# Raw projection weights in two places of their own, and a slab's first down rows loaded when its last pair begins

## The chip, the cores and the metric

The kernel runs on one core of a Trainium2 chip. A core has five engines that run side by side and meet only through semaphores: TensorE (PE in the profile; its weight loads are PEld), VectorE (DVE), ScalarE (ACT), GpSimd (POOL) and SyncE (SP), which here issues all loads and stores. Data moves between the chip's main memory and the on-chip memory (128 partitions) by DMA. The metric is the device time of one execution in microseconds (us). Times are medians of several executions. The profile is one more execution, taken with the hardware profiler.

## What is computed

Two identical layers (DEPTH = 2) over 512 tokens of 1024 channels. Each layer is a gated feed-forward block, a mixer and a second feed-forward block, each followed by a layer norm:

```python
def _swiglu(x, wg, wu, wd):
    return (jax.nn.silu(x @ wg) * (x @ wu)) @ wd
...
    for l in range(DEPTH):
        h = 0.5 * _swiglu(x, ffn_w_gate[l, 0], ffn_w_up[l, 0], ffn_w_down[l, 0])
        x = _layernorm(ALPHA * x + h, ln_g[l, 0], ln_b[l, 0])
        h = _mixer(x, w_in[l], ...)
        x = _layernorm(ALPHA * x + h, ln_g[l, 1], ln_b[l, 1])
        h = 0.5 * _swiglu(x, ffn_w_gate[l, 1], ffn_w_up[l, 1], ffn_w_down[l, 1])
        x = _layernorm(ALPHA * x + h, ln_g[l, 2], ln_b[l, 2])
```

`wg` and `wu` are 1024 x 2816 and `wd` is 2816 x 1024. The mixer projects with `w_in` (1024 x 1792), runs a convolution branch, a recurrent branch and windowed attention, and projects back with `w_out` (1024 x 1024). All in float32.

## The kernel before

**Split numbers.** TensorE is fed float32r values. To keep float32 accuracy every operand is split into a high and a low part (`split`, lines 128 to 132: ScalarE casts the high part at L131, VectorE subtracts it from the source at L132), and every product is three matmuls: low weight by high data, high by low, high by high.

**The feed-forward block** (`ffn`, L465) runs over 22 blocks of 128 hidden channels, two of them making a *pair*, so 11 pairs, in three *slabs* of 4, 4 and 3 pairs (`SLABS`). A pair (class `Pair`, L397) multiplies gate and up weights by the transposed activations in a scheme with seven products instead of eight, so it has seven *steps* named p1, p2, q6, p5, p7, p4 and q3. Each step needs its own combination of the four raw quarters of the pair's weights: `prep` (L428) forms sums t1 to t4 on VectorE (L420) where needed and splits the result. `prep` runs AHEAD = 3 steps in front of the step that is computed. The list `seq` (L551 to L555) puts p4 and q3 of one pair behind p1 of the next, so that after p1 of the last pair of a slab come eight steps: p4 and q3 of the pair before, then p2, q6, p5, p7, p4 and q3 of the last pair. The results end in `hH` and `hL` (`finish`, L492).

When a slab's pairs are done, its *down rows* follow (L578 to L581): for every hidden block f of the slab, `load_rows` loads 128 rows of `wd` (512 KB), splits them, and 24 matmuls of 512 columns (four tiles of tokens, six each, `rowmm`, L454) add to eight PSUM banks. The last slab of a block treats its last four rows (`RESIDENT`) differently: they stay on chip and are used tile by tile in `tail` (L311), which also runs the layer norm (`norm_a`, `norm_b`) and transposes the new activations for the next phase (`to_xT`). So a block has three changes from pairs to down rows, and there are four blocks: twelve changes, four of them in a last slab.

**Places.** A tile pool has a fixed number of places of one tile each, here 128 x 1024 float32. `wpool` has 15 places that serve everything tagged "w": the raw weights that `fetch_raw` (L364) loads, the split halves `wh` and `wl`, the sums t1 to t4, the two result tiles `oa` and `ob` of a pair, and four tiles of the mixer. `load` (L369) asks for raw, high and low, in that order. A raw tile's place comes free when VectorE has subtracted (L132). The pairs' raw quarters (L409) lie in another pool, `tpool`, with 7 places. `fetch_raw` serves the down rows, the mixer's `w_in` and `w_out`, and the first four weight tiles of every block or mixer, which the phase before loads through `nxt.load` (L590 to L592 and in the mixer's end).

**Order.** Tile, the framework, orders the instructions of each engine when the program is built: mostly in program order, but an instruction whose operands and place are there can be put ahead of earlier ones that still wait. Places of one tag are handed out in program order. On the chip every engine then runs its list strictly in order, and SP is one such list: a load whose place is not free holds up every load behind it.

Of the kernel before, what the change touches and what calls it, by code (L numbers as in the profile page):

```python
# [11 lines left out]
F32 = mybir.dt.float32  # L12
# [6 lines left out]
P = 128  # L19
D = 1024  # L20
# [31 lines left out]
def tile_hymba(  # L52
# [26 lines left out]
    nc = tc.nc  # L79

    cpool = ctx.enter_context(tc.tile_pool(name="cpool", bufs=1))
    wpool = ctx.enter_context(tc.tile_pool(name="wpool", bufs=15))
    hpool = ctx.enter_context(tc.tile_pool(name="hpool", bufs=1))
    xpool = ctx.enter_context(tc.tile_pool(name="xpool", bufs=1))
    tpool = ctx.enter_context(tc.tile_pool(name="tpool", bufs=7))
# [6 lines left out]
    def nm(s):  # L92
        uid[0] += 1
        return f"{s}_{uid[0]}"

    def bank():
        return psum.tile([P, 512], F32, tag="ps", name=nm("ps"))
# [36 lines left out]
    def transposed(dst, q, j, src):  # L134

        pt = bank()
        for c in range(4):
            nc.tensor.transpose(pt[:, c * P:(c + 1) * P], src[:, c * P:(c + 1) * P], ident)  # L138
        sl = slice(j * P, j * P + P)
        split(dst[q][:, 0, :, sl], dst[q][:, 1, :, sl], pt.rearrange("p (c t) -> p c t", c=4))  # L140
# [179 lines left out]
    class Start:  # L320
# [6 lines left out]
        def load(self, n=1, pool=None):  # L327
            for _ in range(n):
                self.pairs.append(self.thunks.pop(0)(pool))
# [32 lines left out]
                    mm(pb[:, lo:hi], wh[:, k, :], mh, False, k == KC - 1)  # L362

    def fetch_raw(src):  # L364
        raw = wpool.tile([P, D], F32, tag="w", name=nm("raw"))
        nc.sync.dma_start(raw if len(src.shape) == 2 else raw.rearrange("p (k f) -> p k f", k=KC), src)
        return raw

    def load(src, pool=None, raw=None):  # L369
        raw = fetch_raw(src) if raw is None else raw  # L370
        if pool is None:
            hi = wpool.tile([P, D], F32R, tag="w", name=nm("wh"))
            lo = wpool.tile([P, D], F32R, tag="w", name=nm("wl"))
        else:
            hi = tpool.tile([P, D], F32R, tag="t", name=nm("wh"))
            lo = tpool.tile([P, D], F32R, tag="t", name=nm("wl"))
        split(hi, lo, raw)
        return hi, lo
# [5 lines left out]
        pair = load(cols(src, c), pool, raw)  # L384
        return [w.rearrange("p (k f) -> p k f", k=KC) for w in pair]

    def load_rows(src, c, pool=None):
        return load(src[c * P:(c + 1) * P, :], pool)

# [62 lines left out]
    def rowmm(ys, a, w, first, last):  # L454
        ah, al = a
        wh, wl = w
        for hf in range(2):
            sl = slice(hf * 512, (hf + 1) * 512)
            mm(ys[hf], al, wh[:, sl], first, False)
        for hf in range(2):  # L460
            sl = slice(hf * 512, (hf + 1) * 512)
            mm(ys[hf], ah, wl[:, sl], False, False)
            mm(ys[hf], ah, wh[:, sl], False, last)

    def ffn(l, i, idx, start, nxt, last, hooks={}):  # L465
        wd = w_down[l, i]
# [8 lines left out]
        def product(step, n, pb, first):  # L475
            src, q = A[step]
            wh, wl = pairs[n].ready.pop(step)
            for g in range(2):
                o = pb[:, g * HALF:(g + 1) * HALF]
                for k in range(4):  # L480
                    st = first and g == 0 and k == 0
                    nc.tensor.matmul(o, wl[:, g, k, :], src[q][:, 0, k, :], start=st, stop=False, skip_group_check=True)  # L482
                    nc.tensor.matmul(o, wh[:, g, k, :], src[q][:, 1, k, :], start=False, stop=False, skip_group_check=True)  # L483
                    nc.tensor.matmul(o, wh[:, g, k, :], src[q][:, 0, k, :], start=False, stop=k == 3, skip_group_check=True)  # L484

        for si, (n0, n1) in enumerate(SLABS):
            fin = si == len(SLABS) - 1
            f0, f1 = 2 * n0, 2 * n1
# [3 lines left out]
            def finish(n, which, tile_, s0):  # L492

                v = tile_.rearrange("p (b g s) -> p b g s", b=2, g=2)
                nc.scalar.activation(v[:, :, 0, :], v[:, :, 0, :], AF.Silu)
                nc.vector.tensor_tensor(v[:, :, 0, :], v[:, :, 0, :], v[:, :, 1, :], op=ALU.mult)  # L496
                f = 2 * (n - n0)
                sl = (slice(None), slice(f, f + 2), slice(s0, s0 + HALF))
                split(hH[sl], hL[sl], v[:, :, 0, :])

            def run(step, n):
                if step in ("p1", "p2", "p5"):
                    acc[step, n] = bank()
                pb = acc[{"p1": "p1", "q6": "p1", "p7": "p1", "p4": "p1", "p2": "p2", "p5": "p5", "q3": "p5"}[step], n]
                product(step, n, pb, step in ("p1", "p2", "p5"))
                if step == "p1":
                    outs[n] = [wpool.tile([P, D], F32, tag="w", name=nm("o")) for _ in range(2)]
                oa, ob = outs[n]
                lo, hi = slice(0, 512), slice(512, 1024)
                if step == "p1":  # L510
                    nc.scalar.copy(oa[:, lo], pb)  # L511
                elif step == "p2":
                    nc.vector.tensor_tensor(oa[:, lo], pb, oa[:, lo], op=ALU.add)
                    acc.pop(("p2", n))
                elif step == "q6":
                    nc.scalar.copy(oa[:, hi], pb)
                elif step == "p7":
                    nc.scalar.copy(ob[:, hi], pb)  # L518
                    nc.vector.tensor_tensor(ob[:, hi], acc["p5", n], ob[:, hi], op=ALU.subtract)
                elif step == "p4":  # L520
                    nc.scalar.copy(ob[:, lo], pb)
                    finish(n, 1, ob, HALF)
                elif step == "q3":
                    nc.vector.tensor_tensor(oa[:, hi], pb, oa[:, hi], op=ALU.subtract)
                    finish(n, 0, oa, 0)
                    acc.pop(("p5", n))
                    acc.pop(("p1", n))
                    outs.pop(n)
# [28 lines left out]
            for m, (step, n) in enumerate(seq):  # L557
                while ready < min(len(seq), m + 1 + AHEAD):
                    st, k = seq[ready]
                    pairs[k].prep(st)  # L560
                    ready += 1
                    if st == "p5" and k + 1 < n1:
                        pairs[k + 1].raw(0, 0)
                        pairs[k + 1].raw(1, 0)
                run(step, n)
                if m4:
                    transposed(sT, 2, 2 - len(m4), m4.pop(0))
                if step == "q3" and n in hooks:
                    hooks[n]()
# [4 lines left out]
            def hpair(f, t):  # L574
                return hH[:, f - f0, t * P:(t + 1) * P], hL[:, f - f0, t * P:(t + 1) * P]

            flow = f1 - RESIDENT if fin else f1
            for f in range(f0, flow):  # L578
                w = load_rows(wd, f)
                for t in range(NT):  # L580
                    rowmm(ys[t], hpair(f, t), w, f == f0, f == f1 - 1)  # L581
            if not fin:
# [4 lines left out]
                continue  # L587
            coef = ln_coef(idx)
            ws = [load_rows(wd, f) for f in range(flow, f1)]
            if nxt:  # L590
                nxt.load(3)
# [9 lines left out]
    def mixer(l, idx, start, nxt):  # L601
# [305 lines left out]
        for u in range(U + 2):  # L907
            if u < U:
                scores(u)
            if u < 2:  # L910
                query(2 + u)
            if SLAB_FROM <= u < SLAB_FROM + 4:
                wo.append(load_rows(w_out[l], 4 + u - SLAB_FROM))
            if 0 <= u - 2 < U:
                weighted(u - 2)
            if u - 3 in closes:
                attn_out(closes[u - 3], wo)
            if 0 <= u - 1 < U:
                transpose_p(u - 1)
            point()  # L920
            if u < U:
                normalise(u)
# [7 lines left out]
    for l in range(DEPTH):  # L930
        phases += [(ffn, (l, 0, 3 * l), ffn_start(l, 0)), (mixer, (l, 3 * l + 1), mixer_start(l)),
                   (ffn, (l, 1, 3 * l + 2), ffn_start(l, 1))]
# [61 lines left out]
```

## Time and profile before

| what | us |
|---|---|
| median of 3 executions | 1774.04 (1771.74 to 1775.43) |
| profiled execution, its own time | 1780.14 |
| its span on the core | 1778.4 |
| TensorE busy | 1720.0 (97% of the span) |
| VectorE busy | 1278.1 (72%) |
| ScalarE busy | 821.1 (46%) |
| loads and stores, mean rate | 100 GB/s |
| granted TensorE clock, mean | 0.987 |

Matmuls are pipelined: a matmul's shown duration is longer than its distance to the next one, and its end is modelled. Waits of TensorE are therefore read from the starts of its instructions. In the views of the trace a row of the timeline has the start, the duration, engine, line, operation, written tile and read tiles, and in brackets the engine's idle time before it with what ended it. A row of the waits has the total in us, the number of times and the longest. A row of the windows has the window, its length, each engine's busy time and count, the granted clock, the share of the DMA engines' time and the rate.

### The profile page before, as it was taken

Reading aid. Unit: us, or ns where it says so; the run is one execution under the profiler, and the core shown is the slowest. Engines: PE = TensorE matmul, PEld = TensorE weight load, DVE = VectorE, ACT = ScalarE, POOL = GpSimd, SP = SyncE. Lnnn points to the kernel's source line nnn. Section 1 sums busy time; section 2 is a strip of 40 time slices with the busy share of each in tenths; the row PEclk is TensorE's granted clock in tenths of the full one; section 3 lists DMA queues with packets and bytes.
Section 4 is the critical chain, followed back from the end, with each engine's and each line's share of the span. In section 5 each row is a group of like instructions: output and inputs, shape, how many; then the busy total and the mean of one; then the engine's idle time right before and its main releaser. Section 6 shows DMA issues by size and latency. Waiting matters only on the chain. (4 is left out here: it accounts for less than half of the span.)

```text
span 1778.4 us, 27912 instructions
## 1 busy us (share of the span) xinstructions
PE 1720.0 (97%) x11538; PEld 1546.7 (87%) x11538; DVE 1278.1 (72%) x1777; ACT 821.1 (46%) x1224; POOL 44.0 (2%) x76
## 2 busy tenths in 40 slices
PE   8999999999999999999999999999999999999997
PEld 8988989887679989979889899898875799898896
DVE  5856856779877856747688567576898877577485
ACT  4543533543854543434445335254457445255252
POOL 0200000010000000000000000000000000000000
PEclk9999999999899999999999999999998999999999
DMA  5341542321222432422324324223311244235122
GB/s 157 109 142 57 167 135 72 119 81 45 98 84 75 127 131 72 129 85 72 107 84 131 131 71 128 87 72 110 111 59 58 73 124 144 65 104 163 45 94 72
DMA packets 236840, 177.34 MB, mean 100 GB/s; under 512 B 9524, under 2 KB 219561, under 8 KB 236713
## 3 DMA queue, kind: packets, MB, share of 16 engines
q1 hardware_dynamic: 236712, 175.55, 32.1%
q8 instruction: 91, 1.49, 0.3%
q14 instruction: 37, 0.30, 0.0%
HBM read 171.33 MB, written 3.67 MB: 98 GB/s over the span
## 5 line engine op out<-in xcount | busy, mean ns | idle before, releaser
L132 DVE TENSOR_TENSOR wl<-raw,wh 128x1024 fp32r<-128x1024 f32 x268 | 324.9, 1221 | 156.3 <-ACT wh L131 114.2
L482 PE MATMUL ps<-xT,wl 128*128 128x256 f32 x1280 | 355.5, 278 | 10.8 <-ACT o L518 9.8
L483 PE MATMUL ps<-xT,wh 128*128 128x256 f32 x1280 | 353.3, 276 | 0.0
L484 PE MATMUL ps<-xT,wh 128*128 128x256 f32 x1280 | 353.2, 276 | 0.0
L131 ACT CAST wh<-raw 128x1024 fp32r<-128x1024 f32 x268 | 278.5, 1048 | 132.7 <-DMA raw<-in_ffn_w_down_dram 69.8
L132 DVE TENSOR_TENSOR wl<-t,wh 128x1024 fp32r<-128x1024 f32 x160 | 195.8, 1226 | 143.4 <-ACT wh L131 117.7
L106 PE MATMUL ps<-wl,hH 128*128 128x512 f32 x704 | 276.5, 393 | 4.2 <-DVE wl L132 4.2
L106 PE MATMUL ps<-wh,hH 128*128 128x512 f32 x704 | 275.5, 391 | 0.0
L482 PE MATMUL ps<-sT,wl 128*128 128x256 f32 x960 | 264.8, 276 | 4.9 <-ACT o L511 4.9
L484 PE MATMUL ps<-sT,wh 128*128 128x256 f32 x960 | 264.1, 275 | 0.0
L483 PE MATMUL ps<-sT,wh 128*128 128x256 f32 x960 | 264.1, 275 | 0.0
L131 ACT CAST wh<-t 128x1024 fp32r<-128x1024 f32 x160 | 167.6, 1055 | 201.2 <-DVE t L420 166.0
L482 PEld LDWEIGHTS ps<-xT,wl 128*128 128x128 f32 x1280 | 241.2, 188 | 15.2 <-ACT o L518 12.1
L483 PEld LDWEIGHTS ps<-xT,wh 128*128 128x128 f32 x1280 | 241.3, 188 | 0.3
L484 PEld LDWEIGHTS ps<-xT,wh 128*128 128x128 f32 x1280 | 241.1, 188 | 0.0
L106 PE MATMUL ps<-wh,hL 128*128 128x512 f32 x704 | 218.6, 392 | 4.7 <-ACT wh L131 4.7
L106 PE MATMUL ps<-xT,wh 128*128 128x256 f32 (+1 forms) x960 | 214.3, 318 | 2.2 <-DVE xT L132 2.2
L482 PEld LDWEIGHTS ps<-sT,wl 128*128 128x128 f32 x960 | 180.3, 188 | 6.6 <-ACT o L511 5.8
L484 PEld LDWEIGHTS ps<-sT,wh 128*128 128x128 f32 x960 | 180.2, 188 | 0.0
L483 PEld LDWEIGHTS ps<-sT,wh 128*128 128x128 f32 x960 | 180.2, 188 | 0.0
L106 PEld LDWEIGHTS ps<-xT,wh 128*128 128x128 f32 x960 | 159.2, 191 | 17.1 <-DVE xT L132 3.2
L106 PEld LDWEIGHTS ps<-wl,hH 128*128 128x128 f32 x704 | 132.9, 189 | 35.2 <-DVE wl L132 7.7
(165 smaller groups left out, 2345.7 us busy)
## 6 DMA issues: line engine op xcount, KB each, us to landing
raw<-in_ffn_w_down_dram SPq DMA_DIRECT2D x88, 512.0 KB
raw<-in_ffn_w_gate_dram SPq DMA_DIRECT2D x160, 256.0 KB
raw<-in_ffn_w_up_dram SPq DMA_DIRECT2D x160, 256.0 KB
raw<-in_w_in_dram SPq DMA_DIRECT2D x28, 512.0 KB
raw<-in_w_out_dram SPq DMA_DIRECT2D x16, 512.0 KB
raw<-in_ffn_w_gate_dram SPq DMA_DIRECT2D x8, 512.0 KB
raw<-in_ffn_w_up_dram SPq DMA_DIRECT2D x8, 512.0 KB
t<-in_ln_g_dram SPq DMA_DIRECT2D x6, 512.0 KB
```

What stands on the lines that cost most here:

```text
L106: nc.tensor.matmul(o, a, b, start=start, stop=stop)
L131: nc.scalar.copy(hi, src)
L132: nc.vector.tensor_tensor(lo, src, hi.bitcast(F32), op=ALU.subtract)
L482: nc.tensor.matmul(o, wl[:, g, k, :], src[q][:, 0, k, :], start=st, stop=False, skip_group_check=True)
L483: nc.tensor.matmul(o, wh[:, g, k, :], src[q][:, 1, k, :], start=False, stop=False, skip_group_check=True)
L484: nc.tensor.matmul(o, wh[:, g, k, :], src[q][:, 0, k, :], start=False, stop=k == 3, skip_group_check=True)
```

## The change

Raw weights that `fetch_raw` loads get a pool `rpool` with two places of their own (tag "r"). `wpool` grows from 15 to 16 places and no longer holds them. When a slab's last pair comes to its step p1, the raw tiles of the slab's first two down rows are asked for, before p1's matmuls in program order; `load_rows` takes such a tile where there is one. All other loads keep their place in the program.

```diff
-    wpool = ctx.enter_context(tc.tile_pool(name="wpool", bufs=15))
+    wpool = ctx.enter_context(tc.tile_pool(name="wpool", bufs=16))
+    rpool = ctx.enter_context(tc.tile_pool(name="rpool", bufs=2))
...
     def fetch_raw(src):
-        raw = wpool.tile([P, D], F32, tag="w", name=nm("raw"))
+        raw = rpool.tile([P, D], F32, tag="r", name=nm("raw"))
         nc.sync.dma_start(raw if len(src.shape) == 2 else raw.rearrange("p (k f) -> p k f", k=KC), src)
         return raw
...
-    def load_rows(src, c, pool=None):
-        return load(src[c * P:(c + 1) * P, :], pool)
+    def load_rows(src, c, pool=None, raw=None):
+        return load(src[c * P:(c + 1) * P, :], pool, raw)
...
+                if (step, n) == ("p1", n1 - 1):
+                    first_raw = {f: fetch_raw(wd[f * P:(f + 1) * P, :]) for f in (f0, f0 + 1)}
                 run(step, n)
...
             for f in range(f0, flow):
-                w = load_rows(wd, f)
+                w = load_rows(wd, f, None, first_raw.pop(f, None))
```

## The prediction

> **What bounds the kernel now.** I read the page first, then the waits, then the chain and the timelines around the changes from pairs to down rows.
>
> ```profile
> span 1778.4 us, 27912 instructions
> ...
> PE 1720.0 (97%) x11538; PEld 1546.7 (87%) x11538; DVE 1278.1 (72%) x1777; ACT 821.1 (46%) x1224; POOL 44.0 (2%) x76
> ```
>
> TensorE is the bound, so a change that leaves its matmuls alone can only win what it waits: 58.4 us by these rows (1778.4 - 1720.0), somewhat more by starts, as ends are modelled late. The waits of PE, by what ended them:
>
> ```profile
> PE ps L482 <- ACT o L518: 9.8, 12, 1.7
> PE ps L138 <- DVE xs L306: 6.7, 5, 1.6
> ...
> PE ps L106 <- ACT wh L131: 4.7, 7, 2.1
> PE ps L106 <- DVE wl L132: 4.2, 8, 0.5
> ```
>
> The reader sees four stalls. The first (twelve times, once per slab) is p4 waiting until ScalarE has copied p7's bank. The second is the norm chain ahead of the transposes. The last two, 8.9 us in seven and eight places, are down rows whose weights are not split yet; these the change aims at. The chain at one of them, the second slab of the last block (start, us, what):
>
> ```profile
> 1623.44 2.37 DVE wl L132 x2
> 1625.83 0.37 SPq L412
> ...
> 1626.29 3.75 DMA raw<-in_ffn_w_down_dram
> 1630.06 1.06 ACT wh L131
> 1631.14 1.24 DVE wl L132
> 1632.42 43.37 PE ps L106 x190
> ```
>
> The load of the first down row is issued only at 1626.29, behind a pair load (L412) of the *next* slab that waited in SP's list for VectorE. Then load, cast and subtraction follow one another, 3.75 + 1.06 + 1.24 us, and the pairs' matmuls are over before.
>
> **Term 1: the stall at the change.** In a last slab there is none; compare starts (PE, last pair matmul and first row matmul with a low weight):
>
> ```profile
> 337.67 0.28 PE L484 MATMUL ps<-sT,wh 128*128 128x256 f32 x1
> ...
> 338.25 0.40 PE L106 MATMUL ps<-wl,hH 128*128 128x512 f32 x1
> ```
> ```profile
> 101.39 0.28 PE L484 MATMUL ps<-sT,wh 128*128 128x256 f32 x1
> ...
> 103.80 0.50 PE L106 MATMUL ps<-wl,hH 128*128 128x512 f32 x1 [0.53 <-DVE wl L132]
> ```
> ```profile
> 753.93 0.28 PE L484 MATMUL ps<-sT,wh 128*128 128x256 f32 x1
> 756.31 0.73 PE L106 MATMUL ps<-wh,hL 128*128 128x512 f32 x2 [2.10 <-ACT wh L131]
> 757.57 0.79 PE L106 MATMUL ps<-wl,hH 128*128 128x512 f32 x1 [0.53 <-DVE wl L132]
> ```
> ```profile
> 1630.42 0.28 PE L484 MATMUL ps<-sT,wh 128*128 128x256 f32 x1
> ...
> 1632.42 0.50 PE L106 MATMUL ps<-wl,hH 128*128 128x512 f32 x1 [0.53 <-DVE wl L132]
> ```
>
> The distance is 0.58 us in the last slab and 2.41, 3.64 and 2.00 us in the first, the worst and the last of the eight others; in order the eight are 2.41, 1.84, 1.52, 3.64, 1.70, 2.10, 1.70, 2.00, together 16.9. Less 8 x 0.58 that is **12.3 us**; the wait rows, 8.9, are the lower end.
>
> Does it go? The two raw places are idle through the pairs (pairs load into `tpool`), so nothing on chip holds the two loads back, and SP issues what has a place long before its turn:
>
> ```profile
> 13.95 0.58 SPq L189 DMA_DIRECT2D sink<-in_attn_sinks_dram  x1
> ```
> ```profile
> 189.39 0.31 SPq L180 DMA_DIRECT2D t<-in_conv_dw_w_dram  x1
> ```
>
> Both belong to `load_params`, after pair 5. The one with a place of its own went at 14 us, the other waited for a pool place until 189. So I expect the down loads well ahead of the last pair. Cast and subtraction then need two places of the 16: while q3 is split, at most four split pairs (p5, p7, p4, q3) and `oa`, `ob` are live, 10, so six are free and two rows take four. The nearest rows are those of the last slab, whose raw was early:
>
> ```profile
> 332.04 1.05 ACT L131 CAST wh<-raw 128x1024 fp32r<-128x1024 f32 x1
> ```
> ```profile
> 333.62 1.21 DVE L132 TENSOR_TENSOR wl<-raw,wh 128x1024 fp32r<-128x1024 f32 x1
> ```
>
> Split by 334.83, used at 337.8: 3 us to spare. I take the whole 12.3. What is late next is only L518's wait in each slab, which stays.
>
> **The other down rows** now go through two raw places instead of up to four loads at once. A place turns in about 3.75 + 1.06 + 1.24 = 6.1 us, two places give a row every 3.0 us, and PE takes 43.37 / 190 x 24 = 5.5 us per row. Hidden, at no cost; it would cost from 11 us per turn on.
>
> **Term 2: the norm chain.** At the end of a block four loads for the next phase share places with the resident rows, and their subtractions stand in VectorE's list between the norms:
>
> ```profile
> 883.86 0.69 DVE L290 SCALAR_TENSOR_TENSOR t<-ps,xs 128x512 f32<-128x512 f32 x1 [12.39 <-PE ps L106]
> ...
> 890.96 1.21 DVE L132 TENSOR_TENSOR wl<-raw,wh 128x1024 fp32r<-128x1024 f32 x1
> ```
> ```profile
> 897.21 0.66 PE L138 MATMUL ps<-ident,xs 128*128 128x128 f32 x4 [1.14 <-DVE xs L306]
> ```
> ```profile
> 903.00 0.41 PE L138 MATMUL ps<-ident,xs 128*128 128x128 f32 x2 [1.65 <-DVE xs L306]
> ```
>
> VectorE idles 12.39 us and then does splits while PE waits for xs. With 16 places for split halves, the eight of the four resident rows and the eight of the next four fit without raw tiles among them, so some splits can move into that idle time. Bounds: nothing, and the 6.7 us of the wait row (three waits like that at 897, two like that at 903). I take the first kind, 3 x 1.14 = **3.4 us**: two splits out of the chain cover it, and the third and fourth raw must still wait for the first two to be split.
>
> **Term 3: the mixer.** Its `w_out` splits may be put earlier, into attention, where VectorE and ScalarE are nearly full:
>
> ```profile
> 447.00:486.00 39.00, 35.94 (x147) 22.55 (x147) 34.09 (x105) 33.45 (x96) 0.00 (x0) 0.87 0.33 110
> ```
>
> Here VectorE is busy 34.09 of 39 us. Four of the later splits could enter, at about 1.2 us of VectorE each: at worst 2 mixers x 4 x 1.2 = +9.6 us; two leaving would give about -5. I take 0, as nothing in the program's order there changes. The start of the kernel: its third and fourth loads now wait for a raw place; no wait of PE on weights stands in its rows, so 0.
>
> **Sum.** 12.3 + 3.4 = 15.7. Against the profiled execution (1780.14, span 1778.4) that is 1764.4; that execution lies 6.1 us over the median of 1774.04, so the forecast is **1758.3**.
>
> **The clock.** Right after the worst stall the granted clock is low:
>
> ```profile
> 756.60:763.80 7.20, 6.67 (x17) 4.88 (x17) 6.86 (x9) 5.72 (x8) 0.00 (x0) 0.53 0.66 242
> ```
>
> At 0.53 over 7.2 us, 7.2 x 0.47 = 3.4 us are lost; if the stall is the cause, they go too, and the time is 1754.9. The other stalls of this kind show no such loss, and the median may not have it, so the sum leaves it out. The Trainium skill, "TensorE: Matmul & The Clock Gate", section "Why this matters for your kernels", asks for no idle gap over about 3 us. By that rule 2.3 us would be too short and the sum stays at 1758.3; this row speaks rather against it.
>
> **Rivals.**
> - *Tails stay* (VectorE's list keeps its order): 12.3 alone, 1761.7. For it: the idle 12.39 us was there already and not used.
> - *Attention pays* (term 3 at its worst, tails unchanged): 1774.0 - 12.3 + 9.6 = 1771.3. Against it: `w_out` is needed no earlier.
> - *The change does not do what it says*: the two loads stay behind waiting pair loads in SP's list, or their split halves get no place, and the first row is as late as now: 1774.
> - *Slower: the early loads push back the last pair.* They may be issued just ahead of its raw quarters (0,1) and (1,1), on which t1, t2 and q6 hang:
>
> ```profile
> 1607.79 0.50 SPq L412 DMA_DIRECT2D raw<-in_ffn_w_up_dram  x1
> ```
> ```profile
> 1612.58 1.23 DVE L132 TENSOR_TENSOR wl<-t,wh 128x1024 fp32r<-128x1024 f32 x1 [1.12 <-ACT wh L131]
> ```
> ```profile
> 1615.90 0.28 PE L482 MATMUL ps<-sT,wl 128*128 128x256 f32 x1
> ```
> ```profile
> 1626.00:1630.00 4.00, 4.00 (x38) 4.00 (x37) 0.40 (x1) 0.59 (x1) 0.00 (x0) 1.00 0.76 243
> ```
>
> q6's weights are split at 1613.81 and used at 1615.90: 2.1 us to spare. Two rows are 1.05 MB, at 243 GB/s 4.3 us. From 2.1 us of delay on PE waits; at 4.3 it loses 2.2 us in each of 12 slabs, 26 us: 1774.0 - 12.3 + 26 = 1787.7. The Trainium skill, "DMA: Bandwidth & Descriptors", section "Queues, rings and completion order", says that loads from one issuing engine share one ring per DMA engine, taken in ring order; by that a load in front delays the ones behind in full, which speaks for this rival. Against it: SP's rows above, by which loads with a free place go far earlier.
>
> **Chances.** Forecast 0.36 (1758.3); with the clock as well 0.10 (1754.9); tails stay 0.21 (1761.7); attention pays 0.13 (1771.3); no effect 0.10 (1774); slower 0.10 (1787.7). A measurement here tells 0.2%, 3.5 us, from no change: below 1770.5 is faster. Attention paying falls half on either side, so faster 0.73, same 0.17, slower 0.10. The range goes up to 1774, which leaves out the slower case; its low end has both tail waits (6.7), the clock (3.4) and half of what attention could give (2.5): 1774.0 - 12.3 - 6.7 - 3.4 - 2.5 = 1749.
>
> **What would show it.** Right: at all twelve changes the first low-weight row matmul starts about 0.6 us after the last pair matmul; the waits of L106 on `wh` and `wl` fall from 8.9 us to about nothing; the first down loads stand in SP's list ahead of the last pair's last L412; the wait on xs falls from 6.7 to about 3.3 us. Wrong: new waits of L482 on `wl` in a slab's last pair (the collision), PE waits inside attention over the present ones, or row matmuls after the second that wait for `wh`.

## The result and the profile after

The changed kernel takes 1752.0 us (median of 3, 1749.72 to 1752.65) against 1774.04: the ratio is **0.9869 [0.9855, 0.9883]**, 22 us less. The forecast was 1758.3 with a range from 1749 to 1774. The changed kernel's profiled execution took 1749.72 us, its span is 1747.9. In the changed kernel's lines everything behind `fetch_raw` stands one line lower (L107 for L106, L133 for L132, L483 to L485 for the pairs), the mixer three lower.

From the page, the span and the busy times:

```profile
span 1747.9 us, 27899 instructions
...
PE 1701.4 (97%) x11538; PEld 1540.1 (88%) x11538; DVE 1280.6 (73%) x1777; ACT 823.4 (47%) x1224; POOL 42.1 (2%) x76
```

The waits of TensorE (what waited, for what; us in total, times, longest):

```profile
PE ps L483 <- ACT o L519: 9.8, 12, 1.6
PE ps L139 <- DVE xs L307: 9.0, 3, 4.1
PE ps L139 <- DMA xs<-in_x_dram: 6.1, 2, 4.6
PE ps L483 <- ACT o L512: 4.9, 4, 1.2
PE ps L107 <- ACT t L874: 4.8, 10, 0.8
```

Two things are to be seen. The waits of the down rows on `wh` and `wl`, 8.9 us before, are not in the list at all. The wait on xs, which the prediction had falling from 6.7 to 3.3 us, has *risen* to 9.0, in three places in place of five. The timeline of TensorE at the worst change of before (3.64 us there) and at the last one (2.00 us):

```profile
745.86 0.28 PE L485 MATMUL ps<-sT,wh 128*128 128x256 f32 x1
745.97 0.62 PE L107 MATMUL ps<-wh,hL 128*128 128x512 f32 x2
746.43 0.40 PE L107 MATMUL ps<-wl,hH 128*128 128x512 f32 x1
```
```profile
1605.23 0.28 PE L485 MATMUL ps<-sT,wh 128*128 128x256 f32 x1
1605.34 0.62 PE L107 MATMUL ps<-wh,hL 128*128 128x512 f32 x2
1605.80 0.40 PE L107 MATMUL ps<-wl,hH 128*128 128x512 f32 x1
```

From the last pair matmul to the first one with a low row weight it is 0.57 us, at these two and at the ten others. So the eight stalls went in full, 12.3 us. The other 10 us of the medians' 22 came from somewhere else, although the wait that was to pay 3.4 of them grew.

**Where it came from.** The span can be cut at each slab's last pair matmul. Four of the pieces hold the end of a block (its last down rows, the norm, and what follows up to the next first slab); the other nine hold the kernel's start and the changes with the stalls. Worked out from the starts of those matmuls in each trace, in us (e2, e7, e8 and e10 are experiments below; one of e7's six executions took 2886 us at a granted clock of 0.557 and is in none of the figures):

| piece | before | changed | e7 | e8 | e2 | e10 |
|---|---|---|---|---|---|---|
| end of block 1, mixer, slab | 294.4 | 292.2 | 295.4 | 287.8 | 290.1 | 284.5 |
| end of block 2, slab | 126.1 | 124.0 | 126.4 | 122.7 | 122.8 | 121.8 |
| end of block 3, mixer, slab | 295.1 | 290.3 | 293.5 | 287.8 | 287.7 | 284.5 |
| end of block 4 | 44.7 | 40.9 | 45.0 | 40.9 | 40.9 | 40.9 |
| these four | 760.3 | 747.3 | 760.3 | 739.2 | 741.5 | 731.8 |
| the other nine | 1018.1 | 1000.6 | 1001.7 | 1019.1 | 1003.7 | 1003.4 |

The trace also records the granted clock; for some stretches of time it stands at 0.5, here called half-clock stretches. The changed kernel wins 17.5 us in the other nine pieces: 12.3 of stalls and some 5 of clock, as the half-clock stretch of 6.83 us after the worst stall is missing and the one near 173 is 3.4 us shorter. And it wins 12.9 us at the blocks' ends. There (without the kernel's last 10 us) half-clock stretches add up to 23.9 us before and 10.2 after, which is 11.9 and 5.1 us lost at most, so up to 6.8 of the 12.9 can be clock. The plainest of the blocks' ends is the last one, 3.8 us, where no load for a next phase exists. The timeline of VectorE there, the first half of each token tile's first norm step, before and after:

```profile
1755.81 0.69 DVE L290 SCALAR_TENSOR_TENSOR t<-ps,xs 128x512 f32<-128x512 f32 x1 [12.37 <-PE ps L106]
...
1757.03 0.69 DVE L290 SCALAR_TENSOR_TENSOR t<-ps,xs 128x512 f32<-128x512 f32 x1
...
1761.95 0.68 DVE L290 SCALAR_TENSOR_TENSOR t<-ps,xs 128x512 f32<-128x512 f32 x1
```
```profile
1723.17 0.69 DVE L291 SCALAR_TENSOR_TENSOR t<-ps,xs 128x512 f32<-128x512 f32 x1 [5.05 <-PE ps L107]
...
1728.62 0.69 DVE L291 SCALAR_TENSOR_TENSOR t<-ps,xs 128x512 f32<-128x512 f32 x1 [0.19 <-PE ps L107]
...
1734.06 0.69 DVE L291 SCALAR_TENSOR_TENSOR t<-ps,xs 128x512 f32<-128x512 f32 x1 [0.17 <-PE ps L107]
```

Before, tiles 0 and 1 come 1.2 us apart, 22 us after the last pair matmul (1733.70). After, the tiles come 5.4 us apart and the first is there 16.2 us after that matmul (1706.97). TensorE's order says why. Before, it took the last four rows of tile 0 and tile 1 mixed: the last matmuls into their four banks start 21.7 to 23.0 us after the last pair matmul, so both ended late and their norms stood in a bunch. After, it finishes tile 0 (15.8 and 16.2 us), then tile 1 (21.2 and 21.7 us), and so on; the norm of one tile runs under the matmuls of the next. Nothing in the diff says so: the order comes out of the framework's planner. The experiments below show that it turns with the two early loads in the last slab (e8), and with the own places alone as well (e1). Why the planner mixed the tiles before (it may have held the last weights for late) is argued, not shown.

So after the comparison there were three things to test: the stalls, the order of the last rows, and why the wait on xs had grown. The rival was that own places, the early load and the 16th place each had a share.

### The profile page after: what moved, and what is told of

Its sections match the earlier page's. It is cut to its first block, busy times and chain, and to the rows that moved or that the text cites. A ratio compares the mean times of both kernels' runs of the same rounds, so it can differ in the third digit from the quotient of the medians.

```text
span 1747.9 us, 27899 instructions
## 1 busy us (share of the span) xinstructions
PE 1701.4 (97%) x11538; PEld 1540.1 (88%) x11538; DVE 1280.6 (73%) x1777; ACT 823.4 (47%) x1224; POOL 42.1 (2%) x76
## 4 chain that ended last, share of the span: by engine, by line
PE 70%; DVE 15%; ACT 7%; DMA 5%; issue 2%; SPq 0%; POOL 0%; DVEq 0%; ACTq 0%; POOLq 0%
PE ps L107 41%; PE ps L483 9%; PE ps L485 9%; PE ps L484 9%; DVE wl L133 5%; DVE t L421 4%; ACT wh L132 4%; DMA raw<-in_ffn_w_up_dram 2%; PE ps L139 2%; DMA raw<-in_ffn_w_down_dram 1%; ACT t L845 1%; DVE o L497 1%; DVE hL L133 1%; DMA raw<-in_w_in_dram 1%; DVE o L525 1%
## 5 line engine op out<-in xcount | busy, mean ns | idle before, releaser
L133 DVE TENSOR_TENSOR wl<-raw,wh 128x1024 fp32r<-128x1024 f32 x268 | 324.5, 1221 | 136.2 <-ACT wh L132 135.5
L483 PE MATMUL ps<-xT,wl 128*128 128x256 f32 x1280 | 355.3, 278 | 10.8 <-ACT o L519 9.8
L485 PE MATMUL ps<-xT,wh 128*128 128x256 f32 x1280 | 353.0, 276 | 0.0
L132 ACT CAST wh<-raw 128x1024 fp32r<-128x1024 f32 x268 | 277.6, 1049 | 157.0 <-DMA raw<-in_ffn_w_down_dram 90.6
L133 DVE TENSOR_TENSOR wl<-t,wh 128x1024 fp32r<-128x1024 f32 x160 | 195.8, 1226 | 136.7 <-ACT wh L132 136.6
L107 PE MATMUL ps<-wl,hH 128*128 128x512 f32 x704 | 275.6, 391 | 0.0
L132 ACT CAST wh<-t 128x1024 fp32r<-128x1024 f32 x160 | 168.3, 1054 | 226.8 <-DVE t L421 194.4
L107 PE MATMUL ps<-wh,hH 128*128 128x512 f32 x704 | 275.1, 391 | 0.0
L483 PE MATMUL ps<-sT,wl 128*128 128x256 f32 x960 | 264.6, 276 | 4.9 <-ACT o L512 4.9
L485 PE MATMUL ps<-sT,wh 128*128 128x256 f32 x960 | 264.1, 275 | 0.0
L483 PEld LDWEIGHTS ps<-xT,wl 128*128 128x128 f32 x1280 | 241.0, 188 | 14.7 <-ACT o L519 12.1
L485 PEld LDWEIGHTS ps<-xT,wh 128*128 128x128 f32 x1280 | 241.0, 188 | 0.0
L107 PE MATMUL ps<-wh,hL 128*128 128x512 f32 x704 | 218.9, 392 | 0.0
L107 PE MATMUL ps<-xT,wh 128*128 128x256 f32 (+1 forms) x960 | 211.8, 316 | 0.0
L483 PEld LDWEIGHTS ps<-sT,wl 128*128 128x128 f32 x960 | 180.2, 188 | 6.4 <-ACT o L512 5.8
L485 PEld LDWEIGHTS ps<-sT,wh 128*128 128x128 f32 x960 | 180.2, 188 | 0.0
L107 PEld LDWEIGHTS ps<-xT,wh 128*128 128x128 f32 x960 | 157.4, 189 | 13.9 <-issue 0.5
L107 PEld LDWEIGHTS ps<-wl,hH 128*128 128x128 f32 x704 | 133.0, 189 | 27.9
```

The source lines that it names most:

```text
L107: nc.tensor.matmul(o, a, b, start=start, stop=stop)
L132: nc.scalar.copy(hi, src)
L133: nc.vector.tensor_tensor(lo, src, hi.bitcast(F32), op=ALU.subtract)
```

## The experiments

All were run beside the kernel before, with ratios to it and 95% intervals.

**Own places without the early load (e1).**

```diff
-                if (step, n) == ("p1", n1 - 1):
-                    first_raw = {f: fetch_raw(wd[f * P:(f + 1) * P, :]) for f in (f0, f0 + 1)}
...
-                w = load_rows(wd, f, None, first_raw.pop(f, None))
+                w = load_rows(wd, f)
```

> After, with the two lines taken out that load a slab's first two down rows when its last pair begins; raw tiles keep two places of their own, 16 shared. Theory (places): a free place of its own is enough, the load goes as soon as SP's list lets it, so the twelve changes stay at 0.57 us and the time is that of the changed kernel, -22 us, ratio 0.987 (0.986 to 0.988). Rival (early load): the line is what brings the rows early; then the 12.3 us of stalls come back and only the tails remain better, -4 to -8 us, ratio 0.996 to 0.998.

Measured: 0.9875 [0.9861, 0.9889], all twelve distances 0.57 us. TensorE's matmuls have the lines, tiles and shapes of the changed kernel's, one by one, and the last block's end takes the same 40.9 us. The early load is no cause of anything here: with a place of its own the load goes as soon as SP's list has none before it that waits. The timeline of SP at the first slab of the last block shows how far ahead, first in the *changed* kernel (two rows), then in e1:

```profile
1481.10 21.53 SPq L367 DMA_DIRECT2D raw<-in_ffn_w_down_dram  x8
1505.75 0.38 SPq L413 DMA_DIRECT2D raw<-in_ffn_w_gate_dram  x1
```
```profile
1479.96 21.77 SPq L367 DMA_DIRECT2D raw<-in_ffn_w_down_dram  x8
```

Eight loads in a row: six of this slab, whose first two were there, and two of the *next* slab, which are needed at 1605. The last pair that the early load is tied to begins near 1580 (e2, next), so in the changed kernel the line asks for loads that were issued some 80 us ahead of it, and without the line they go as early.

**The early load without own places (e2).** Before's 15 shared places; against the changed kernel:

```diff
-    wpool = ctx.enter_context(tc.tile_pool(name="wpool", bufs=16))
-    rpool = ctx.enter_context(tc.tile_pool(name="rpool", bufs=2))
+    wpool = ctx.enter_context(tc.tile_pool(name="wpool", bufs=15))
...
-        raw = rpool.tile([P, D], F32, tag="r", name=nm("raw"))
+        raw = wpool.tile([P, D], F32, tag="w", name=nm("raw"))
```

> Before, with only the early load: a slab's first two raw down rows are loaded when its last pair begins, out of the 15 shared places. Theory (a load that stands ahead in SP's list is all that is needed): no stall at the twelve changes, -12.3 us, and the last down rows of a block go through TensorE token tile by token tile as in the changed kernel, another -4 to -6 us: ratio 0.988 to 0.991. Rival (places): six tiles more live in the last pair's time in 15 places hold back the splits of the pair; new waits of L482 to L484 on wl or wh, part of the gain lost, ratio 0.993 or more. Second rival (both parts needed for the whole): 0.987 is not reached because the mixers keep their form of before.

Measured: 0.9835 [0.9818, 0.9851], the stalls gone (0.57 us twelve times), nearly no new wait of the pairs on `wl` (1.4 us in five places, 1.0 in four before). The ratio is lower than the 0.988 to 0.991 expected, as the blocks' ends win more than the 4 to 6 us that were put down for them. In this kernel the early load does work; the timeline of SP, 22 us ahead of the change at 1602.7, behind the last load of the last pair:

```profile
1579.88 0.64 SPq L412 DMA_DIRECT2D raw<-in_ffn_w_up_dram  x1
1580.61 0.93 SPq L366 DMA_DIRECT2D raw<-in_ffn_w_down_dram  x2
1582.33 0.38 SPq L412 DMA_DIRECT2D raw<-in_ffn_w_gate_dram  x1
```

So either half of the change removes the stalls alone, and this half with *less* memory is faster than the whole change. Its waits of TensorE have no row for xs:

```profile
PE ps L482 <- ACT o L518: 9.0, 12, 1.2
PE ps L138 <- DMA xs<-in_x_dram: 6.0, 2, 4.6
PE ps L106 <- ACT t L873: 5.1, 5, 1.3
PE ps L482 <- ACT o L511: 4.9, 4, 1.2
```

**The early load in eight slabs, and in the other four (e7, e8).** As e2, with a condition more in e7; e8 has `and fin` there:

```diff
-                if (step, n) == ("p1", n1 - 1):
+                if (step, n) == ("p1", n1 - 1) and not fin:
```

> As e2_early, but the early load is made in the eight slabs that are not the last of their block; TensorE's whole list of matmuls is then that of before, one by one. Theory: the eight stalls go, 12.3 us, and nothing else; the last tail stays at 44.7 us from last pair matmul to end. -12.3 us, ratio 0.9931; with the half clock after the worst stall, where it follows from the stall, -15.7 us, ratio 0.9912. Rival (the tails' gain comes from free places in SP's list and not from the order of the rows): the tails get shorter here as well and the time comes near e2_early.

> As e2_early, but the early load is made only in the four last slabs of the blocks, where no stall stood. Theory (order of the last rows): TensorE takes the four last rows of token tile 0 before those of tile 1, the first norm starts some 6 us earlier and the norms no longer come in a bunch; the eight stalls stay. Last tail 44.7 to 41 us, -3.8 us, with the tail between the blocks -2.1 us more: -4 to -6 us, ratio 0.9966 to 0.9979. Rival (the tails' gain comes from the raw tiles' own places, since no raw tile stands between the splits there): ratio 0.999 to 1.000.

Measured: e7 0.9926 [0.9912, 0.9940], 13.1 us; e8 0.9918 [0.9906, 0.9931], 14.6 us. The table above splits them cleanly. In e7 TensorE's list is that of before, the blocks' ends take what they took (760.3 us) and the rest falls by 16.4. In e8 the stalls stay (14.1 us over 0.58 each, 12.3 before), the rest stays, and the blocks' ends fall by 21.1; its last one is the changed kernel's, 40.9 us. The wait on xs has gone with the early load in the last slabs alone: e8 has no row for it. It isn't the order of the rows that removes it, as the changed kernel takes them tile by tile too and has 9.0 us of it. The direction was as expected, the size was not: 14.6 us where 4 to 6 were expected. Together they make 27.7 us, and e2, which does both, 29.3 (26.5 to 32.3).

How much of this is clock can be estimated: an execution's span times its granted clock leaves out what the clock lost. The median of that product is 1759.3 us in the eleven executions of before beside these runs, 1747.3 in e7 and 1749.8 in e8. So e7 wins 12.0 us without the clock, close to the 12.3 of the stalls, and e8 9.5; some 5 of e8's 14.6 us are clock, and the 9.5 are still more than was expected. (The clock is on record with three digits, which is up to 0.9 us in the product.)

**More shared places, nothing else (e9), and the early load with 18 (e4).** The changed kernel has 18 places in all. The edit, against before for e9 and against e2 for e4:

```diff
-    wpool = ctx.enter_context(tc.tile_pool(name="wpool", bufs=15))
+    wpool = ctx.enter_context(tc.tile_pool(name="wpool", bufs=18))
```

> Before, with 18 shared places in place of 15: the memory of the changed kernel and neither its own places nor its early load. Theory (what counts is that a load stands ahead in SP's list with a place free then, and that no raw tile of the next phase lacks a place at a block's end; more places in the common ring leave the list of loads at a slab's change as it is): the eight stalls stay near 12 us, TensorE's list is that of before, ratio 0.998 to 1.000. Rival (three more places do it): ratio 0.990 or less.

> e2_early with 18 shared places in place of 15: the early load with the changed kernel's memory, and no places of its own for raw tiles. Theory (memory is not what is short; what counts at a block's end is how many raw tiles may be loaded and split before the first norm): a time like e2_early's, ratio 0.983 (0.981 to 0.985), no wait of L106 on wh or wl, no wait on xs over 1 us. Rival (e10_r4 with its 18 places is faster only because it has three more than e2_early): ratio 0.978 as e10_r4.

Measured: e9 1.0001 [0.9988, 1.0013], stalls 14.2 us; e4 0.9832 [0.9808, 0.9856]. More shared places win nothing, neither without the early load nor with it.

**The block's end from the shared places (e5), and more places of their own (e11, e10, e12).** In e5 `fetch_raw` takes a place of `wpool` while `shared` has something in it:

```diff
+            shared.append(1)
             ws = [load_rows(wd, f) for f in range(flow, f1)]
             if nxt:
                 nxt.load(3)
                 nxt.load(1, None)
+            shared.pop()
```

The others differ from the changed kernel in two numbers, 3 and 15 in e11, 4 and 14 in e10 (shown), 5 and 13 in e12:

```diff
-    wpool = ctx.enter_context(tc.tile_pool(name="wpool", bufs=16))
-    rpool = ctx.enter_context(tc.tile_pool(name="rpool", bufs=2))
+    wpool = ctx.enter_context(tc.tile_pool(name="wpool", bufs=14))
+    rpool = ctx.enter_context(tc.tile_pool(name="rpool", bufs=4))
```

> After, but the raw tiles that are loaded at the end of a block (its four last down rows, the four pairs of the next phase) come from the 16 shared places again; all others keep the two places of their own. Theory (two places turn too slowly at a block's end: a load, a cast and a subtraction each, and VectorE's list has the late splits between the steps of the first norm): the wait of TensorE on xs, 9.0 us in three places in the changed kernel, goes as it is gone in e2_early (none); TensorE's order of the last rows stays; about -7 to -9 us against the changed kernel, ratio 0.983 (0.981 to 0.985). Rival (e2_early is faster because the pairs' and the mixer's raw tiles share, or by chance of the clock): the time stays that of the changed kernel, 0.987, with the waits on xs gone or not.

> After, with three places of their own for raw tiles and 15 shared ones (18 in all, as before). Theory (two are too few at a block's end): the splits of the next phase's first pairs stand in VectorE's list ahead of the first norm, in its idle time, and the wait on xs falls from 9.0 us to under 1 us; -8 us against the changed kernel, ratio 0.983. Rival (places of their own are the trouble, not their number): waits on xs stay at 7 to 9 us, ratio 0.987.

> After, with four places of their own for raw tiles and 14 shared ones (18 in all). Theory as for three: waits on xs under 1 us, ratio 0.983, and one shared place less costs nothing that shows. Rival: 14 shared places are too few for the last pair's splits with two down rows, new waits of L483 to L485 on wl or wh, ratio 0.986 or more.

> After, with five places of their own for raw tiles and 13 shared ones. Theory: all that a block's end wants ahead is there with four; nothing more to win, ratio 0.977 to 0.979. Rival (13 shared places are too few for the last pair): new waits of L483 on wl or wh, ratio 0.980 or more.

Measured: e5 0.9809 [0.9794, 0.9825]; three places 0.9795 [0.9781, 0.9810], four **0.9778 [0.9762, 0.9794]**, five 0.9780 [0.9760, 0.9800]. None of the four has a wait on xs. Three and four came out better than the 0.983 expected, e5 just below its range. Four has the lowest ratio, 1737.56 us beside 1777.4 of before on its chip; three and five can't be told from it by these intervals.

Why two are too few is seen in the changed kernel's longest wait on xs. First TensorE's transposes, then ScalarE, then VectorE:

```profile
359.27 1.11 PE L139 MATMUL ps<-ident,xs 128*128 128x128 f32 x4 [4.14 <-DVE xs L307]
```
```profile
353.72 1.05 ACT L132 CAST wh<-raw 128x1024 fp32r<-128x1024 f32 x1 [2.61 <-DMA raw<-in_w_in_dram]
...
356.25 1.04 ACT L132 CAST wh<-raw 128x1024 fp32r<-128x1024 f32 x1 [0.34 <-DMA raw<-in_w_in_dram]
```
```profile
353.87 0.75 DVE L305 SCALAR_TENSOR_TENSOR xs<-t,nmean,t 128x512 f32<-128x512 f32 x1
354.80 1.22 DVE L133 TENSOR_TENSOR wl<-raw,wh 128x1024 fp32r<-128x1024 f32 x1 [0.18 <-ACT wh L132]
355.94 0.74 DVE L305 SCALAR_TENSOR_TENSOR xs<-t,nmean,t 128x512 f32<-128x512 f32 x1
357.32 1.23 DVE L133 TENSOR_TENSOR wl<-raw,wh 128x1024 fp32r<-128x1024 f32 x1 [0.64 <-ACT wh L132]
358.47 1.41 DVE L307 SCALAR_TENSOR_TENSOR xs<-xs,rs,t 128x512 f32<-128x512 f32 x2
```

The next phase's raw tiles wait for one of two places, arrive late (ScalarE idles 2.61 us for one), and the subtractions of two of them stand in VectorE's list between the steps of tile 0's norm. VectorE runs its list in order, so the norm waits for a cast that waits for a load. ScalarE's square for the norm stands behind such a cast too. With four places the same stretch of VectorE's timeline is free of splits:

```profile
352.87 1.42 DVE L305 SCALAR_TENSOR_TENSOR xs<-t,nmean,t 128x512 f32<-128x512 f32 x2
355.06 1.42 DVE L307 SCALAR_TENSOR_TENSOR xs<-xs,rs,t 128x512 f32<-128x512 f32 x2 [0.78 <-POOL rs L298]
356.71 0.69 DVE L291 SCALAR_TENSOR_TENSOR t<-ps,xs 128x512 f32<-128x512 f32 x1 [0.23 <-PE ps L107]
```

From the norm's first step on xs to its last it is 4.6 us in the changed kernel (353.87 to 358.47) and 2.2 us here.

**A filling for the one big wait that is left (e6, e13).** p4 waits for ScalarE's copy of p7's bank, 9 to 10 us in 12 places. Six matmuls of the first down row need neither that bank nor p4's weights:

```diff
+                if (step, n) == ("p4", n1 - 1):
+                    ys0 = [bank(), bank()]
+                    w0 = load_rows(wd, f0, None, first_raw.pop(f0))
+                    rowmm(ys0, hpair(f0, 0), w0, True, False)
                 run(step, n)
```

e13 asks for `w0` before p7 instead, on the kernel with four own places.

> e2_early, with the six matmuls of the first down row on token tile 0 moved from behind the last pair to a place ahead of its p4, in all twelve slabs. They need neither the pair's bank nor its weights, and take 1.4 us where TensorE now waits 0.75 us for ScalarE's copy of p7 (9.0 us in 12 places). Theory: that wait goes, -7 to -9 us against e2_early, ratio 0.9785 to 0.980. Rival: the first down row's weights are not split yet some 6 us earlier than they are used now; TensorE waits for wh or wl at that place instead, and nothing or less than half is won: 0.982 to 0.985.

> e10_r4, with the first down row's cast and subtraction asked for ahead of p7 of the last pair, and its six matmuls on token tile 0 put ahead of p4, where TensorE waits 10.2 us in 12 places for ScalarE's copy of p7. In e6_fill the cast stood behind that copy in ScalarE's list and the wait stayed. Theory: the wait on L519's copy goes from 10.2 to under 2 us, and the rows behind the pair do not wait in its place: -7 to -9 us against e10_r4, ratio 0.973 to 0.9745. Rival (a bank that the rows of the last token tiles need comes free late, as 4.5 us of L106 on L524 in e6_fill show): half of it or less, ratio 0.9755 to 0.978.

Neither won anything. e6: 0.9871 [0.9854, 0.9888], slower than its base e2 by about 6 us. The planner put the six among p4's matmuls, behind the first ones (that it saw their weights late is argued), and the wait stayed (9.0 us in 12 places), with 4.5 us of L106 on L524's bank added. e13: 0.9869 [0.9849, 0.9889], 16 us slower than its base. The wait on L519 has left the list, and this stands in its place:

```profile
PE ps L107 <- ACT wh L132: 13.4, 12, 2.2
...
PE ps L107 <- DVE wl L133: 4.9, 11, 0.4
```

These two rows make 18.3 us where 10.2 went; the rest of the 16 us isn't broken down. At the first such place ScalarE and VectorE split the weights of p4, q3 and the row one behind the other, and TensorE reaches the row's before the split is done. The rival that had been written down, the late bank, was not the main one: L107 waits 0.7 us for it. Whether a split a step earlier (before q6) would fit wasn't tried.

## Why the prediction was right, and where its steps were not

The time lies inside the range, and the largest term was right. That the sum came within 6.3 us is in part luck: its second term failed, and the blocks' ends won by a mechanism that the prediction didn't have.

- **Term 1, the stall at the change, 12.3 us:** right in mechanism and size. Twelve distances of 0.57 us; e7 shows it alone (13.1 us, 12.0 without the clock).
- **The early load well ahead of the last pair:** the consequence held, the reason given was half right. The prediction had it from SP's rows that a load with a place goes early; by that reason the line in `ffn` is not needed, and e1 shows that it isn't.
- **Other down rows through two places, no cost:** held. No row of L107 waits for `wh` or `wl`.
- **Term 2, the norm chain, 3.4 us from the wait on xs:** this step failed. It took for granted that two own places let the next phase's splits move into VectorE's idle time. Two of the four at the first block's end do; the other two stand inside tile 0's norm, and the wait on xs rose from 6.7 to 9.0 us. Its own caveat, that "the third and fourth raw must still wait for the first two to be split", was the mechanism, and should have been priced against it. With three or four places no wait on xs is left.
- **What the sum left out: TensorE's own order.** The blocks' ends win 12.9 us in the profiles all the same, at least 6.1 of them without the clock; the last rows go tile by tile. The prediction treated the order of the matmuls as given. e8 shows that it changes with the loads; with the splits that move along with it, this is worth 14.6 us alone, 9.5 without the clock.
- **Term 3, the mixer, 0:** right in size, not in its reason. The splits of `w_out` did move: before, VectorE subtracts for them at 463.87, 470.82 and 479.44, in the changed kernel at none between 459.9 and 486.6. Attention's length in the first mixer can be read between its first and its eighth `es` on VectorE, in before, in the changed kernel and in e8, whose splits stand as before:

```profile
453.92 0.16 DVE L839 TENSOR_TENSOR es<-nm,sink 128x4 f32<-128x4 f32 x1
...
502.76 0.16 DVE L839 TENSOR_TENSOR es<-nm,sink 128x4 f32<-128x4 f32 x1
```
```profile
449.93 0.16 DVE L842 TENSOR_TENSOR es<-nm,sink 128x4 f32<-128x4 f32 x1
...
495.62 0.16 DVE L842 TENSOR_TENSOR es<-nm,sink 128x4 f32<-128x4 f32 x1
```
```profile
451.40 0.15 DVE L842 TENSOR_TENSOR es<-nm,sink 128x4 f32<-128x4 f32 x1
...
497.34 0.16 DVE L842 TENSOR_TENSOR es<-nm,sink 128x4 f32<-128x4 f32 x1
```

  It takes 48.8 us before, 45.7 in the changed kernel and 45.9 in e8. Before has a half-clock stretch of 10.24 us in it, the other two have none. So the moved splits are worth some 0.3 us, and the rest is the clock.

- **The rivals.** "Tails stay" (1761.7) was wrong on both sides: one part of the tail won, another lost. "Attention pays" didn't come (45.7 us against 45.9). "No effect" fell with the first timeline. The slower one, the early loads just in front of the last pair's, never had its condition: in the changed kernel they go far earlier, and in e2 right behind the last pair's last load (1580.61 behind 1579.88). The wait of the pairs on `wl` is 1.0 us in four places as before, and 1.4 in e2. What loads just in front would cost is not shown.
- **The clock:** the half-clock stretch after the worst stall is gone, in the changed kernel and in e7. That the stall was its cause isn't shown: e8 and e9 keep this stall (3.30 and 3.29 us against 3.64) and have no half-clock stretch behind it, while e8 has one of 3.41 us behind a stall of 2.94 us. The sum without the clock was 6.3 us above the result. The product of span and granted clock is 1739.7 us in the changed kernel's three executions (median; 1740.0 in e1), 19.6 less than the 1759.3 of before, where the sum had 15.7. So, as an estimate, some 4 of the 6.3 us are the blocks' ends, and the rest is the clock. It varies between executions: before's ran from 0.986 to 0.995 over the runs beside the experiments, with 1784 to 1770 us.

## What to carry to other kernels

A transfer that is late because it stands behind a waiting one in its queue needs a free place of its own (e1) or an earlier stand in that queue (e2); more places in the common pool won nothing (e9). Count what else will queue for the new place, and give a pool of its own as many as its longest burst wants ahead (here three or four, not two). Where a planner writes the engines' lists, a change of loads changes the order of the matmuls too: compare the lists, and cut the time at fixed points of the work, before crediting a gain to the wait it was meant for.

## What was not expected of the hardware

The same waits of TensorE are followed by a loss of clock in one profile and not in another. Before, in the second mixer, it had two waits of under 1 us within 3 us, and so has e8 at the same place (first before, then e8):

```profile
1348.85 1.12 PE L106 MATMUL ps<-t,mix 128*128 128x512 f32 x2 [0.82 <-ACT t L871]
1350.94 0.69 PE L867 MATMUL ps<-ident,t 128*128 128x128 f32 x2 [0.97 <-DVE t L857]
```
```profile
1347.50:1361.20 13.70, 11.92 (x30) 6.19 (x28) 10.88 (x39) 10.97 (x35) 0.00 (x0) 0.63 0.12 38
```
```profile
1333.51 1.13 PE L106 MATMUL ps<-t,mix 128*128 128x512 f32 x2 [0.81 <-ACT t L874]
1335.60 0.44 PE L870 MATMUL ps<-ident,t 128*128 128x128 f32 x2 [0.97 <-DVE t L860]
```
```profile
1331.00:1346.00 15.00, 12.29 (x52) 7.68 (x51) 12.90 (x44) 13.62 (x43) 0.00 (x0) 1.00 0.13 48
```

The granted clock of before's window is 0.63; its record stands at half from 1350.9 on for 10.24 us, 5.1 us lost at most. In e8's window it is 1.00. Long waits differ in the same way: in the changed kernel the clock stands at half for 6.83 us from 357.1 on, 2.0 us into the wait of 4.14 us that ends at 359.27; e1 has a wait of 3.61 us at the same place (ended at 361.55) and a granted clock of 1.00 from 357 to 372. So neither the length of one wait nor two short ones in a row decides alone in these profiles, and what does stays open. The Trainium skill, "TensorE: Matmul & The Clock Gate", section "Why this matters for your kernels", warns of one gap over about 3 us; the 4.14 us agree with it, the 3.61 us of e1 don't, and before's loss comes without such a gap. The same page, section "A second HAM failure mode: psum-queue depth-cycling", has a kernel that loses clock to frequent short idle times; before's second mixer would fit that, e8's doesn't. All half-clock stretches inside TensorE's work, in the profiles of before and after, are 3.41, 6.83 or 10.24 us long, which are one to three of the 3413 ns windows that the page gives (section "What's actually happening"). One near 172 us is in every profile, with no wait of TensorE over 0.2 us in the 15 us ahead of it. It begins 3 to 6 us after the first of 16 matmuls that make the table of position biases (`ps<-t,t`, 33 rows of the 128, float32), in all fourteen profiles; whether these matmuls are its cause wasn't tested.
